# A two-layer transformer forward pass on one core: the 32-row block exchange moved from GpSimd's to SyncE's queue, the first x tiles loaded in halves, and the chunk states computed alternately in two banks

## The chip, the cores and the metric

The kernel runs on one core of a Trainium2 chip. The metric is the device time of one execution in microseconds (us), lower is better. TensorE is PE in the profile (PEld are its weight loads), VectorE is DVE, ScalarE ACT, GpSimd POOL, SyncE SP.

## The reference

Two transformer blocks over 256 tokens of width 2048, in float32. The first has an attention with a forget gate and a feed-forward network with a causal convolution of width 3. The second has gated linear attention (GLA, 4 heads, chunks of 64 tokens) and dilated attention (8 heads) side by side, and a gated feed-forward network of width 5632. Cut to what matters here:

```
def first_block(x, ...):
    h = x
    a = rms_norm(h, mix_norm)
    h = h + fox_mixer(a, ...)            # 16 heads: softmax(q k^T * scale + cum_i - cum_j) v, then @ w_out
    return h + conv_ffn(rms_norm(h, ffn_norm), ...)

def second_block(x, ...):
    h = rms_norm(x, norm1_g)
    qa, ka, va, ra, ga, qb, kb, vb = split(h @ w_in)
    mix = concat([gla_mixer(qa, ka, va, ra, log_g), dilated_mixer(qb, kb, vb)])
    x = x + mix @ w_out
    h2 = rms_norm(x, norm2_g)
    return x + (silu(h2 @ w_gate) * (h2 @ w_up)) @ w_down

# in gla_mixer, per head and chunk n of 64 tokens:
chunk_state[n] = k_dec[n]^T @ v[n]                      # 128 x 256
state[n] = decay[n] * state[n-1] + chunk_state[n]
```

## The kernel before, in words

**Products.** Every large product `x @ w` is made by `gemm` for one block of 512 output columns at a time. Weights come in tiles of 1 MB (4 x 128 input rows by 512 columns). `dma_to` loads them on SP's queue into `raw`, which has three buffers (NRAW). `split_to` turns half a tile (a unit) into a rounded high part `wh` (ACT, L105) and the rest `wl` (DVE, L111), in five buffers (NSPL), four units ahead of the product (LEAD). Each unit is 12 matmuls of 128x512 on PE (L118 to L120: high by high, low by high, high by low, for two blocks of 128 tokens and two of 128 input rows). A block with 2048 input rows is 8 units, 96 matmuls.

**Order.** Everything is written out in program order, engine by engine: after each unit `gemm` calls `pump`, which advances generators by one `yield`. An evacuation (`resid`, `plain`, `conv_evac`, `up_evac`) is such a generator; attention and GLA (`attention`, `gla`) run in a second list. Each engine works through its instructions in that order, and the splits of `split_to` stand four units ahead of PE's products among them.

**Block exchange.** Products give tokens on partitions, and the next product needs features there. Where `flip` is used, DVE first transposes blocks of 32x32 (`turn`, L312); one `yield` later `exchange` writes `turn` to DRAM in four stores of 128 KB (`way`, L303); another `yield` later one load of 512 KB brings it back with the blocks exchanged (L318). Four yields later ACT reads the result (L328). `turned` does the same for two heads' attention weights (`pturn`). These DMAs are issued by POOL. POOL also puts the residual `h` away to DRAM and fetches it (`home`), loads the gate sums (`cum_dram`, `ckb`) and does part of the head norms (L241, L242, L392) and of the attention bias (L656 to L661).

**Residual blocks.** `resid` adds the product to `h` (DVE, L347), and for the first three of four blocks flips it and splits it for the next product (`r`, L105 and L111). The fourth block is transposed by PE (`tp`, L290). On ACT and DVE the split of block n's flip stands ahead of the add of block n + 1.

**Start.** x comes transposed in four tiles of 512 KB (`xr`), each scaled and split into `x` by `prep_x` (ACT L107, DVE L113) before the weight units that use it. Tile 0 is loaded and prepared in quarters. For tiles 1 to 3 `load_x` fetches the whole tile ahead of its weight tile.

**Chunk states.** In `gla`, for n = 0, 1, 2, four float32 matmuls (one per head) with 64 rows of contraction make `cs`; n = 0 and n = 2 use partitions 0 to 63 of `kd` and `v`, n = 1 partitions 64 to 127. Each n is one step of the pump, with two PSUM tiles of two heads each.

Of the kernel before, what the change touches and what calls it, by code (L numbers as in the profile page):

```python
# [18 lines left out]
P = 128  # L19
D = 2048  # L20
S = 256
# [22 lines left out]
def fox_gla_dilated_kernel(  # L44
# [36 lines left out]
    def alloc(shape, dt, name):  # L81
        i = free_slots.popleft()
        t = slots.tile([P] + shape, dt, tag=f"s{i}", name=name)
        slot_of[id(t)] = (i, t)
        return t
# [53 lines left out]
    def dma_to(i):  # L139
        while next_dma[0] <= min(i, len(plan) - 1):  # L140
            k = next_dma[0]
            t = rawp.tile([P, 4, 512], F32, tag="raw", name="raw")
            src = plan[k].rearrange("p (k c) -> p k c", c=512)
            if k == 0:
                for q in range(4):
                    nc.sync.dma_start(out=t[:, q], in_=src[:, q])
            else:
                if k < KG:
                    load_x(k)
                if k < 3:  # L150
                    for q in (slice(0, 2), slice(2, 4)):
                        nc.sync.dma_start(out=t[:, q], in_=src[:, q])
                else:
                    nc.sync.dma_start(out=t, in_=src)
                if k == 3:
                    nc.sync.dma_start(out=cols[:, C_FFN:], in_=cols_d[:, C_FFN:])
                    nc.sync.dma_start(out=wn, in_=w_n.rearrange("p (a k c) -> p a k c", a=2, c=16))
                if k == 8:
                    nc.sync.dma_start(out=const, in_=const_d)
                if 4 <= k < 8:  # L160
                    fetch(k - 4, nc.sync)
            raw_t[k] = t
            next_dma[0] += 1

    def split_to(u, mid=None):
        while next_spl[0] <= min(u, 2 * len(plan) - 1):
            k = next_spl[0]
            dma_to(k // 2 + NRAW - 1)
            if k in (2, 4, 6):
                prep_x(k // 2)  # L170
            r = raw_t[k // 2][:, (k % 2) * 2:(k % 2) * 2 + 2]
            wh = splp.tile([P, 2, 512], F32R, tag="wh", name="wh")
            wl = splp.tile([P, 2, 512], F32R, tag="wl", name="wl")
            if k < 2:
                for q in range(2):
                    if mid:
                        mid(2 * k + q)
                    hi_of(wh[:, q], r[:, q])
                    lo_of(wl[:, q], r[:, q], wh[:, q])
            else:  # L180
                hi_of(wh, r)
                lo_of(wl, r, wh)
            spl_t[k] = (wh, wl)
            if k % 2:
                raw_t.pop(k // 2)
            next_spl[0] += 1
# [81 lines left out]
    wn = cpool.tile([P, 2, 16, 16], F32, name="wn")  # L268
    gqk = cpool.tile([P, 2], F32, name="gqk")

    def load_x(i, kt=None):
        src = x_t[i].rearrange("p (k c) -> p k c", c=S)
        if kt is None:
            nc.sync.dma_start(out=xr[i], in_=src)
        else:
            nc.scalar.dma_start(out=xr[i][:, kt], in_=src[:, kt])

    rows = {}

# [20 lines left out]
    def exchange(turn, width):  # L300
        way = ways.tile([P, 4, S], F32, tag="way", name="way")
        for i in range(4):
            nc.gpsimd.dma_start(out=way[:, i, 0:width].rearrange("(j c) e -> c j e", c=32),  # L303
                              in_=turn[32 * i:32 * i + 32, :, 0:width])
        return way[:, :, 0:width]

    def flip(src, into=None):
        turn = alloc([4, S], F32, "turn")
        sv = src.rearrange("p t (k q c) -> p t q k c", q=4, c=32)
        qv = turn.rearrange("p q (k t r) -> p t q k r", t=2, r=32)  # L310
        for t in range(2):
            dve.transpose(out=qv[:, t], in_=sv[:, t])  # L312
        yield
        way = exchange(turn, S)
        yield
        held = alloc([4, S], F32, "flip") if into is None else into
        f = held.rearrange("p a c -> p (a c)").rearrange("p (i e) -> p i e", i=4)
        nc.gpsimd.dma_start(out=f, in_=way)  # L318
        for _ in range(4):
            yield  # L320
        return f.rearrange("p i (k t r) -> p k t i r", k=4, t=2), held, turn
# [93 lines left out]
    def attention(box, gqk, bias_of, ot, done, tag, flipped, ready=None):  # L415
# [58 lines left out]
        def turned(pairs):  # L474
            held = {}
            for a in pairs:
                turn = alloc([4, S], F32, "pturn")
                for n in range(2):
                    pb = sm.pop(a + n)
                    dve.transpose(  # L480
                        out=turn[:, :, n * 96:(n + 1) * 96].rearrange("p j (c r) -> p j c r", c=3),
                        in_=pb[:, 0].rearrange("p (c j r) -> p j c r", c=3, j=4),
                    )
                    free(pb)
                yield
                way = exchange(turn, 192)
                yield
                held[a] = turn
                nc.gpsimd.dma_start(out=turn[:, :, 0:192], in_=way)
            for _ in range(3):  # L490
                yield
            for a in pairs:
                f = held[a][:, :, 0:192].rearrange("p i (n c r) -> p n c i r", n=2, c=3)
                for n in range(2):
                    pt[a + n] = alloc([3, P], F32, "pts")
                    act.copy(pt[a + n].rearrange("p c (i r) -> p c i r", i=4), f[:, n])
                free(held[a])
                yield
# [36 lines left out]
    def run_all():  # L535
# [287 lines left out]
        def gla():  # L823
# [34 lines left out]
            while "v1" not in G:  # L858
                yield
            v = [G["v0"], G["v1"]]  # L860
            st = []
            for n in range(3):
                t, r0 = n // 2, (n % 2) * 64
                s_ = alloc([4, S], F32, "state")
                for pr in range(2):
                    ps = side([2, S], "cs")
                    for kk in range(2):
                        hd = pr * 2 + kk
                        pe.matmul(ps[:, kk], kd[r0:r0 + 64, t, hd * P:(hd + 1) * P],
                                  v[pr][r0:r0 + 64, t, kk * S:(kk + 1) * S], start=True, stop=True)  # L870
                    if n == 0:
                        act.copy(s_[:, pr * 2:pr * 2 + 2], ps)
                    else:
                        for kk in range(2):
                            hd = pr * 2 + kk
                            dve.scalar_tensor_tensor(
                                out=s_[:, hd], in0=st[-1][:, hd], scalar=eb[:, hd, n * 64 + 63:n * 64 + 64],
                                in1=ps[:, kk], op0=ALU.mult, op1=ALU.add)
                st.append(s_)
                yield  # L880
            free(kd)
            o = [alloc([2, 512], F32, f"o{i}") for i in range(2)]
            ssq = small.tile([P, 2, 4], F32, tag="ssq", name="ssq", bufs=1)
# [209 lines left out]
```

## Time and profile before

| | |
|---|---|
| time, median of 3 runs | 2243.42 us (2242.3 to 2247.32) |
| the profiled execution's own time | 2246.22 us |
| its span, first to last instruction | 2244.4 us |
| mean granted TensorE clock | 0.997 |
| PE busy | 2219.1 us (99%) |
| DVE, ACT, POOL busy | 1290.0, 1148.9, 316.3 us |
| DMA: SP's queue (q1), POOL's queue (q0), share of 16 engines | 53.3%, 11.5% |

The last DMA of the span is not part of it, which leaves 1.8 us between the span and the time. PE's busy time counts a matmul from its start to its modelled end, so overlapping matmuls hide short gaps. Where the profile says "DMA to landing", it counts from the issue of a DMA to its last byte's semaphore. The clock is 1.00 for 2.4 GHz and 0.50 for 1.2 GHz.

### The profile page before, as it was taken

How to read it: one execution, taken by the hardware profiler on the slowest of the kernel's cores; microseconds unless marked ns; L12 is line 12 of the kernel's file. 1: busy time of each engine (PE TensorE's matmuls, PEld its weight loads, DVE VectorE, ACT ScalarE, POOL GpSimd, SP SyncE). 2: the span in 40 equal slices, each digit the busy share in tenths (PEclk: the TensorE clock that was granted, in tenths of full speed). 3: DMA queues.
4: the chain of work that ended last, by engine and by line, in shares of the span. 5: the costliest groups of instructions: out<-in, count | busy, mean ns of one | idle time of the engine just before them, and what ended most of it. 6: DMA issues, size and time to landing. Idle time of an engine off the chain costs nothing.

```text
span 2244.4 us, 25865 instructions
## 1 busy us (share of the span) xinstructions
PE 2219.1 (99%) x9888; PEld 1827.7 (81%) x9888; DVE 1290.0 (57%) x1531; ACT 1148.9 (51%) x1565; POOL 316.3 (14%) x483
## 2 busy tenths in 40 slices
PE   9999999899999999999999999999999999999999
PEld 6788888788888888888887887887888888888887
DVE  5656565466767677654555663555555555554443
ACT  6555555466666656544456654544444444444332
POOL 0453321011111111000222320010000000000000
PEclk9999999999999999999999999999999999999999
DMA  7676657677777777666664773585666666676553
GB/s 297 234 252 209 226 194 245 226 234 252 234 242 243 240 245 245 221 232 236 235 217 168 253 250 135 204 279 193 227 217 212 217 225 214 210 245 228 197 203 116
DMA packets 87403, 502.27 MB, mean 224 GB/s; under 512 B 12560, under 2 KB 14272, under 8 KB 37488
## 3 DMA queue, kind: packets, MB, share of 16 engines
q1 hardware_dynamic: 60272, 417.59, 53.3%
q0 software_dynamic: 26144, 82.39, 11.5%
q8 instruction: 77, 1.26, 0.2%
q10 hardware_dynamic: 864, 0.66, 0.1%
q14 instruction: 46, 0.38, 0.1%
HBM read 459.94 MB, written 40.65 MB: 223 GB/s over the span
## 4 chain that ended last, share of the span: by engine, by line
PE 91%; DMA 4%; ACT 1%; POOL 1%; DVE 1%; issue 1%; ACTq 0%; DVEq 0%; POOLq 0%; SPq 0%
PE acc L118 29%; PE acc L120 29%; PE acc L119 29%; DMA way<-turn 2%; DMA flip<-way 1%; POOL way L303 1%; ACT wh L105 1%; PE sc L443 0%; DMA xr<-in_x_t_dram 0%; DMA way<-pturn 0%; ACT turn L328 0%; PE nar L603 0%; DMA ckb<-cum_dram 0%; DVE h L347 0%; PE sc L442 0%
## 5 line engine op out<-in xcount | busy, mean ns | idle before, releaser
L111 DVE TENSOR_TENSOR wl<-raw,wh 128x1024 fp32r<-128x1024 f32 (+1 forms) x786 | 964.6, 1230 | 816.8 <-ACT wh L105 816.3
L105 ACT CAST wh<-raw 128x1024 fp32r<-128x1024 f32 (+1 forms) x786 | 820.5, 1048 | 793.3 <-PE acc L120 758.7
L118 PE MATMUL acc<-wh,r 128*128 128x512 f32 x1792 | 702.1, 392 | 0.0
L120 PE MATMUL acc<-wh,r 128*128 128x512 f32 x1792 | 698.1, 390 | 0.0
L119 PE MATMUL acc<-wl,r 128*128 128x512 f32 x1792 | 698.0, 390 | 0.0
L118 PEld LDWEIGHTS acc<-wh,r 128*128 128x128 f32 x1792 | 337.1, 188 | 72.0 <-issue 2.5
L120 PEld LDWEIGHTS acc<-wh,r 128*128 128x128 f32 x1792 | 336.8, 188 | 70.5
L119 PEld LDWEIGHTS acc<-wl,r 128*128 128x128 f32 x1792 | 336.9, 188 | 69.3
L118 PE MATMUL acc<-wh,g 128*128 128x512 f32 x704 | 273.9, 389 | 0.0
L119 PE MATMUL acc<-wl,g 128*128 128x512 f32 x704 | 273.9, 389 | 0.0
L120 PE MATMUL acc<-wh,g 128*128 128x512 f32 x704 | 273.9, 389 | 0.0
L303 POOL DMA_DIRECT2D way<-turn x216 | 119.5, 560 | 984.0 <-DVE turn L312 909.0
L118 PE MATMUL acc<-wh,x 128*128 128x512 f32 x384 | 154.5, 402 | 1.2 <-ACT wh L105 1.2
L120 PEld LDWEIGHTS acc<-wh,g 128*128 128x128 f32 x704 | 132.1, 188 | 27.6
L119 PEld LDWEIGHTS acc<-wl,g 128*128 128x128 f32 x704 | 132.1, 188 | 27.5
L118 PEld LDWEIGHTS acc<-wh,g 128*128 128x128 f32 x704 | 132.1, 188 | 27.3
L119 PE MATMUL acc<-wl,x 128*128 128x512 f32 x384 | 149.8, 390 | 0.8 <-DVE wl L111 0.8
L120 PE MATMUL acc<-wh,x 128*128 128x512 f32 x384 | 150.0, 391 | 0.0
L118 PEld LDWEIGHTS acc<-wh,x 128*128 128x128 f32 x384 | 72.4, 189 | 16.6 <-ACT wh L105 1.6
L119 PEld LDWEIGHTS acc<-wl,x 128*128 128x128 f32 x384 | 72.5, 189 | 15.9 <-DVE wl L111 1.3
L120 PEld LDWEIGHTS acc<-wh,x 128*128 128x128 f32 x384 | 72.2, 188 | 15.7
L714 DVE SCALAR_TENSOR_TENSOR u<-turn,cols,u 128x255 f32<-128x255 f32 (+1 forms) x176 | 80.9, 481 | 3.1
(212 smaller groups left out, 1470.0 us busy)
## 6 DMA issues: line engine op xcount, KB each, us to landing
raw<-in_w_dram SPq DMA_DIRECT2D x301, 1024.0 KB, 5.0
raw<-in_w7g_dram SPq DMA_DIRECT2D x44, 1024.0 KB, 4.8
raw<-in_w7u_dram SPq DMA_DIRECT2D x44, 1024.0 KB, 5.0
way<-turn POOLq DMA_DIRECT2D x216, 128.0 KB, 4.7
u<-way POOLq DMA_DIRECT2D x22, 512.0 KB, 5.0
home<-h POOLq DMA_DIRECT2D x12, 512.0 KB, 6.6
h<-home POOLq DMA_DIRECT2D x12, 512.0 KB, 8.4
sg<-way POOLq DMA_DIRECT2D x11, 512.0 KB, 5.6
```

Source lines behind the costliest of these rows:

```text
L105: act.copy(out_, in_)
L111: dve.tensor_tensor(out=out_, in0=in_, in1=hi.bitcast(F32), op=ALU.subtract)
L118: pe.matmul(out_, xh, wh, start=first, stop=False)
L119: pe.matmul(out_, xh, wl, start=False, stop=False)
L120: pe.matmul(out_, xl, wh, start=False, stop=last)
L303: nc.gpsimd.dma_start(out=way[:, i, 0:width].rearrange("(j c) e -> c j e", c=32), in_=turn[32 * i:32 * i + 32, :, 0:width])
L714: dve.scalar_tensor_tensor(out=yy[:, d:S], in0=n[:, kt, 0:S - d], scalar=col(C_CW + 176 - 88 * d + ch), in1=yy[:, d:S], op0=ALU.mult, op1= ...
```

## The change

Three edits. The five DMAs of a block exchange (in `exchange`, `flip` and `turned`) are issued by SP instead of POOL. For x tiles 1 and 2 the load is cut in two halves of 256 KB, each issued just ahead of the half of the weight tile that it is used with, and `prep_x` prepares tiles 1 to 3 in halves, each ahead of its unit. In `gla` the states of chunks 0 and 1 are computed together, head by head, alternating between two PSUM tiles, and chunk 2 follows; the pump is still given three steps.

```
             else:
-                if k < KG:
-                    load_x(k)
                 if k < 3:
                     for q in (slice(0, 2), slice(2, 4)):
+                        load_x(k, q, nc.sync)
                         nc.sync.dma_start(out=t[:, q], in_=src[:, q])
                 else:
+                    if k < KG:
+                        load_x(k)
                     nc.sync.dma_start(out=t, in_=src)
...
-            if k in (2, 4, 6):
-                prep_x(k // 2)
+            if 2 <= k < 8:
+                prep_x(k // 2, (0, 1) if k % 2 == 0 else (2, 3))
...
     def exchange(turn, width):
...
-            nc.gpsimd.dma_start(out=way[:, i, 0:width].rearrange("(j c) e -> c j e", c=32),
+            nc.sync.dma_start(out=way[:, i, 0:width].rearrange("(j c) e -> c j e", c=32),
...
-        nc.gpsimd.dma_start(out=f, in_=way)
+        nc.sync.dma_start(out=f, in_=way)
...
-                nc.gpsimd.dma_start(out=turn[:, :, 0:192], in_=way)
+                nc.sync.dma_start(out=turn[:, :, 0:192], in_=way)
...
-            for n in range(3):
-                t, r0 = n // 2, (n % 2) * 64
-                s_ = alloc([4, S], F32, "state")
-                for pr in range(2):
-                    ps = side([2, S], "cs")
-                    for kk in range(2):
-                        hd = pr * 2 + kk
-                        pe.matmul(ps[:, kk], kd[r0:r0 + 64, t, hd * P:(hd + 1) * P],
-                                  v[pr][r0:r0 + 64, t, kk * S:(kk + 1) * S], start=True, stop=True)
...
+            def chunk(ps, n, pr, kk):
+                t, r0, hd = n // 2, (n % 2) * 64, pr * 2 + kk
+                pe.matmul(ps[:, kk], kd[r0:r0 + 64, t, hd * P:(hd + 1) * P],
+                          v[pr][r0:r0 + 64, t, kk * S:(kk + 1) * S], start=True, stop=True)
...
+            for pr in range(2):
+                two = [side([2, S], "cs") for _ in range(2)]
+                for kk in range(2):
+                    for n in range(2):
+                        chunk(two[n], n, pr, kk)
+                act.copy(st[0][:, pr * 2:pr * 2 + 2], two[0])
+                carry(two[1], 1, pr)
+                yield
+            for pr in range(2):
+                ps = side([2, S], "cs")
+                for kk in range(2):
+                    chunk(ps, 2, pr, kk)
+                carry(ps, 2, pr)
+            yield
```

Where the instructions now stand. POOL's queue before the change, where the first attention begins (`q`, `k`: the first group's queries and keys):

```order
L392 TENSOR_TENSOR k<-k,rsh 128x1024
L303 DMA way<-turn 32x4x256 x4
L643 DMA cum_dram<-cumts 16x256
L647 DMA ckb_613<-cum_dram 128x1024
L647 DMA ckb_615<-cum_dram 128x1024
L647 DMA ckb_617<-cum_dram 128x1024
L647 DMA ckb_619<-cum_dram 128x1024
L318 DMA q<-way 128x1024
L303 DMA way<-turn 32x4x256 x4
L318 DMA k<-way 128x1024
```

SP's queue after the change at the same place:

```order
L155 DMA raw<-in_w_dram 128x2048 x4
L304 DMA way<-turn 32x4x256 x4
L155 DMA raw<-in_w_dram 128x2048
L319 DMA q<-way 128x1024
L304 DMA way<-turn 32x4x256 x4
L155 DMA raw<-in_w_dram 128x2048
L319 DMA k<-way 128x1024
```

The exchange of q and k no longer stands behind the gate sums; each exchange now has one 1 MB weight load between its stores and its load back.

SP's queue after the change at the end of the second block's output projection (`flip`: a residual block):

```order
L155 DMA raw<-in_w_dram 128x2048 x3
L304 DMA way<-turn 32x4x256 x4
L155 DMA raw<-in_w_dram 128x2048
L319 DMA flip<-way 128x1024
L155 DMA raw<-in_w_dram 128x2048 x2
L155 DMA raw<-in_w7g_dram 128x2048
L304 DMA way<-turn 32x4x256 x4
L155 DMA raw<-in_w7g_dram 128x2048
L319 DMA flip<-way 128x1024
```

Before the change SP's queue held only the weight loads here, and the `way` and `flip` rows stood on POOL's, in the same order.

PE in the chunk states before (the number behind `cs` is the PSUM tile; the first two of the three steps):

```order
L869 MATMUL cs_10569<-v0_10375,kd_10434 128x256 x2
L869 MATMUL cs_10573<-v1_10545,kd_10434 128x256 x2
L869 MATMUL cs_10594<-v0_10375,kd_10434 128x256 x2
L869 MATMUL cs_10599<-v1_10545,kd_10434 128x256 x2
```

And after, the first of the three steps:

```order
L866 MATMUL cs_10573<-v0_10377,kd_10436 128x256
L866 MATMUL cs_10574<-v0_10377,kd_10436 128x256
L866 MATMUL cs_10573<-v0_10377,kd_10436 128x256
L866 MATMUL cs_10574<-v0_10377,kd_10436 128x256
```

Neighbours now differ in the half of the partitions that they read and in the PSUM tile that they write.

## Rows read from the trace of the kernel before

**Rows 1.** Stretches: length; busy (count) PE, PEld, DVE, ACT, POOL; clock, DMA share, GB/s.

```profile
10.00:40.00 30.00, 28.04 (x123) 21.67 (x122) 19.80 (x26) 19.99 (x33) 0.00 (x0) 1.00 1.02 407
408.40:413.40 5.00, 4.84 (x16) 3.99 (x17) 3.54 (x6) 2.30 (x6) 0.54 (x1) 0.54 0.81 301
1530.00:1900.00 370.00, 370.00 (x1634) 306.39 (x1633) 199.08 (x202) 164.68 (x186) 22.10 (x40) 1.00 0.64 217
```

**Rows 2.** Waits, whole run: who waited for whom; total us, times, longest.

```profile
ACT turn L328 <- DMA q<-way: 13.8, 2, 12.0
PE tp L290 <- DVE h L347: 12.2, 3, 7.6
PE sc L442 <- ACT turn L328: 5.6, 1, 5.6
```

**Rows 3.** Chain that ended last, pieces in order of time: start us, us, what.

```profile
95.82 0.80 PE sc L442 x2
...
97.47 0.43 PE acc L118
...
409.03 1.75 PE tp L290 x7
...
1129.97 0.87 PE tp L290 x8
...
1475.83 1.22 DVE turn L312 x2
...
1492.00 1.71 ACT turn L328 x4
...
1496.87 1.28 DVE h L347 x2
...
1499.28 1.22 DVE turn L312 x2
...
1525.35 0.43 PE acc L120
```

**Rows 4.** DVE's timeline, 62 to 98 us: start, us, instruction, idle before.

```profile
65.35 1.29 DVE L312 STREAM_TRANSPOSE turn<-q 128x512 f32<-128x512 f32 x2
...
70.51 1.29 DVE L312 STREAM_TRANSPOSE turn<-k 128x512 f32<-128x512 f32 x2
```

**Rows 5.** POOL's timeline, same stretch.

```profile
76.98 0.53 POOL L318 DMA_DIRECT2D q<-way  x1
...
81.59 0.55 POOL L303 DMA_DIRECT2D way<-turn  x1 [2.41 <-DMA ckb<-cum_dram]
```

**Rows 6.** DMA issues, whole run: queue, count, KB each, median us to landing.

```profile
out_dram<-h SPq DMA_DIRECT2D x7, 256.0 KB, 2.2
```

**Rows 7.** The weight loads of line 154, 600 to 700 us.

```profile
L154 SPq DMA_DIRECT2D raw<-in_w_dram x18: 327/328/328, 605.1 to 697.9; - x18
...
DMA to landing us min/median/max: 4.7/6.1/7.9
```

**Rows 8.** Chain that ended last, at the start.

```profile
5.15 6.59 DMA xr<-in_x_t_dram
11.77 1.71 ACT x L107 x4
```

**Rows 9.** PE's timeline at the start, 12.4 to 16 us, with idle before.

```profile
14.46 0.49 PE L118 MATMUL acc<-wh,x 128*128 128x512 f32 x1 [1.19 <-ACT wh L105]
15.72 0.50 PE L119 MATMUL acc<-wl,x 128*128 128x512 f32 x1 [0.76 <-DVE wl L111]
```

**Rows 10.** PE's timeline at GLA, 1369 to 1387 us.

```profile
1369.64 1.99 PE L869 MATMUL cs<-v,kd 64*128 64x256 f32 x8
1371.56 0.50 PE L118 MATMUL acc<-wh,r 128*128 128x512 f32 x1
...
1384.36 0.43 PE L891 MATMUL o<-v,at 128*64 128x256 f32 x1
...
1386.24 0.50 PE L118 MATMUL acc<-wh,r 128*128 128x512 f32 x1
```

More of the change, by code (lines that the diff above doesn't have):

```diff
@@ L269, in fox_gla_dilated_kernel, with load_x @@
     gqk = cpool.tile([P, 2], F32, name="gqk")
-    def load_x(i, kt=None):
+    def load_x(i, kt=None, queue=nc.scalar):
         src = x_t[i].rearrange("p (k c) -> p k c", c=S)
@@ L275, in load_x @@
         else:
-            nc.scalar.dma_start(out=xr[i][:, kt], in_=src[:, kt])
+            queue.dma_start(out=xr[i][:, kt], in_=src[:, kt])
     rows = {}
@@ L860, in gla, with carry @@
             v = [G["v0"], G["v1"]]
-            st = []
-            for n in range(3):
-                t, r0 = n // 2, (n % 2) * 64
-                s_ = alloc([4, S], F32, "state")
-                for pr in range(2):
-                    ps = side([2, S], "cs")
-                    for kk in range(2):
-                        hd = pr * 2 + kk
-                        pe.matmul(ps[:, kk], kd[r0:r0 + 64, t, hd * P:(hd + 1) * P],
-                                  v[pr][r0:r0 + 64, t, kk * S:(kk + 1) * S], start=True, stop=True)
[L871 to L879, printed above, removed]
-                yield
+            st = [alloc([4, S], F32, "state") for _ in range(3)]
+            def chunk(ps, n, pr, kk):
+                t, r0, hd = n // 2, (n % 2) * 64, pr * 2 + kk
+                pe.matmul(ps[:, kk], kd[r0:r0 + 64, t, hd * P:(hd + 1) * P],
+                          v[pr][r0:r0 + 64, t, kk * S:(kk + 1) * S], start=True, stop=True)
+            def carry(ps, n, pr):
+                for kk in range(2):
+                    hd = pr * 2 + kk
+                    dve.scalar_tensor_tensor(
+                        out=st[n][:, hd], in0=st[n - 1][:, hd], scalar=eb[:, hd, n * 64 + 63:n * 64 + 64],
+                        in1=ps[:, kk], op0=ALU.mult, op1=ALU.add)
+            for pr in range(2):
[5 more added lines that the diff above has]
+                carry(two[1], 1, pr)
+                yield
+            for pr in range(2):
+                ps = side([2, S], "cs")
+                for kk in range(2):
+                    chunk(ps, 2, pr, kk)
+                carry(ps, 2, pr)
+            yield
             free(kd)
```

## The prediction

> **What bounds the kernel now.** I read the page first, then the windows, the waits, and the chain of waits at each place where PE stands still. The table of the profile has PE busy 99% of the span; in a stretch without a stall 1634 matmuls take 370 us, 0.2264 us each at full clock [rows 1]. So a block of 96 matmuls takes 21.7 us and a unit of 12 takes 2.72 us, and nothing helps that doesn't shorten PE's own work or one of its few waits. The list of waits has two that matter: `tp` waits 12.2 us for the residual add, almost all in two places (7.6 us the longest), and the first `sc` waits 5.6 us for a turned operand [rows 2]. At the start PE waits 1.2 and 0.8 us more [rows 9]. That is all: 19.8 us. What follows a long wait is slow too: after the stall at 400 us the granted clock is 0.54 over 5 us [rows 1], and seven transposes take 1.75 us where eight take 0.87 elsewhere [rows 3].
>
> **The residual blocks (two output projections).** The chain shows a loop that goes round once per residual block. DVE ends the transposes of one at 1475.83 + 1.22 = 1477.05; the blocks are stored and loaded back, and ACT reads them at 1492.00: 15.0 us. From there to the next block's add it is 4.9 us (1496.87: ACT and DVE do the split first), and to the end of the next transposes 3.6 us more (1499.28 + 1.22 = 1500.50) [rows 3]. Together 23.5 us, against 21.7 us of PE's work for a block. So each of three exchanges puts the adds further behind, until PE waits for the last one. The stall goes when exchange and read take less than 21.7 - 4.9 - 3.6 = 13.2 us.
>
> What does SP's queue make of the 15.0? Issuing: four stores at 0.33 us, as SP's loads take [rows 7], 1.3 us. Landing of the stores: at best 2.2 us, as a 256 KB store on SP [rows 6]; at worst they stand behind a whole 1 MB load (4.7 us, the shortest in [rows 7]) and take their own time, 512 KB at 407 GB/s = 1.3 us [rows 1]: 6.0 us. The load back: at best 2.2 + 0.6 for twice the bytes = 2.8 us, at worst again behind the weight load that now stands between, 6.0 us. With two handovers of 0.3 us: 6.9 to 13.9 us. I take 10: at the stores the load ahead has mostly landed (it waits for the DVE split that runs before the transposes), at the load back it has not. That is 18.5 us a round, under 21.7, and only the very top of the range is over it. So both stalls go: 12.2 us.
>
> **The first attention.** Here the order on POOL's queue is late, not the transfer. q's transposes end at 65.35 + 1.29 = 66.6 [rows 4], but POOL issues q's load only at 76.98, after 2 MB of `ckb`, and one store of k waits 2.41 us more for `ckb` [rows 5]. ACT stands 12.0 us at q's load [rows 2], and k's read, on which `sc` hangs, is late. After the change q and k stand on SP between weight loads. q lands by some 66.6 + 10 = 77; k's transposes end at 71.8 [rows 4], plus 10, plus what `ckb` takes from a shared 407 GB/s (at most 2 MB, 5.2 us): 82 to 87, then ACT's four reads, 1.7 us. PE comes to `sc` at 95.82 - 5.6 = 90.2 [rows 2, 3], or 89 with the gain at the start. This fits, with 0.5 to 5 us to spare: 5.6 us. The bounds are 0 (if weights, `ckb` and both exchanges fill the DMAs until 90) and 5.6.
>
> **The clock.** After each of the three stalls PE runs at the lower level for some us. In the chain 11 matmuls there (first at 97.47, last at 1525.35) take 0.43 us in place of 0.23: 2.2 us; the two sets of transposes lose 7 x (0.25 - 0.11) = 1.0 us each [rows 3]. That is 4.2 us, and it goes with the stalls. The bounds are 0 and three times the 5 x 0.46 = 2.3 us that [rows 1] makes of one stall, 6.9.
>
> **The start.** x's tile 1 lands at 5.15 + 6.59 = 11.74, then four ACT operations take 1.71 us before the first weight cast [rows 8]. DMA is full there at 407 GB/s [rows 1], so 512 KB are 1.3 us: half of x lands at 11.1, the first weight half at 12.4 (13.0 before), and two ACT operations are done at 12.0. The cast takes 1.0 us, DVE's rest 1.26 us more (14.46 to 15.72), and L119 starts at 14.7 in place of 15.72 [rows 9]. Gain 1.0 us; between 0.4 (weights land as before) and the whole 2.0. Two more issues on SP cost nothing as long as bytes wait in the queue, which a full DMA shows.
>
> **Chunk states.** One step is 8 records in 1.92 us, 0.24 each (1369.64 to 1371.56); in `o`, whose matmuls alternate between two halves of the output partitions, 12 records take 1.88 us, 0.16 each (1384.36 to 1386.24) [rows 10]. So halves overlap; there it is columns of the array, here it would be rows, which no row of the profile shows. If they do, two of three steps fall to half: 1.9 us less; if not, 0. I take 1.7, since `o` shows it in one direction. "TensorEngine Tiling (Array Packing)" of the Trainium skill, Key Properties, has tiles work independently, and its Gotcha 1 asks for different PSUM banks of different row tiles, which the edit gives; by it the sum would have 1.9. ACT's copy and the carries on DVE stay and have two steps of the pump, 5 us, until `o` needs them.
>
> **What it may cost.** SP now waits in order: behind each load back (until its stores have landed) stands the next weight load. A weight load is issued when the tile three before it is split, 12.4 us ahead of its own split by the code (two tiles of 5.44 us and some 1.5); it lands after 4.7 to 7.9 us [rows 7], so 4.5 to 7.7 us are spare. The split itself runs four units, 10.9 us, ahead of PE and takes 2.3: 8.6 more. I count 15 us of cover. An exchange makes SP wait some 4 us for its stores and puts 1 MB (2.6 us) before weights: under 7 us. With two exchanges in one block (`pturn` and q) it is some 9. It is covered, so 0.
>
> **Sum.** 2246.22 - 12.2 - 5.6 - 4.2 - 1.0 - 1.7 = 2221.5 us, against the profiled execution's own time, which is 2.8 us above the median of the runs shown. On the median's footing 2218.7; I add 1.3 us for short waits that will show where the long ones were (a `tp` that comes just before its add): **2220 us**. This case's own range is 2214 to 2227.
>
> **Rivals.**
> (a) *Part of it stays.* In the first attention the DMAs are too full, or one output projection still stalls. For: `ckb`, two exchanges and the weights fall together. Against: the time to spare. It gives 2220 + 5.6 + 1 (clock) = 2227 or, with the longer `tp` wait, 2220 + 7.6 + 1.5 = 2229; with both 2236.
> (b) *The queue makes no difference.* The exchange takes 15 us on SP as well (stores behind a load, load back behind a load, the top of my range and a little more), and only the start, the chunk states and the order at the first attention help. For: the bytes and the 16 DMA engines stay the same. Against: the direct order. 2220 + 12.2 + 3.4 = 2236, and 2243 if the first attention stays too.
> The Trainium skill's "DMA: Bandwidth & Descriptors", Issuing engines are not separate DMA queues, says that DMAs of all issuers run on the same engines and interleave, so that another issuer saves only the issue time. By it alone (b) is what happens; the trace agrees that the engines are shared, but q's load at 76.98 [rows 5] is late by the order within a queue, which the rule leaves open.
> (c) *Slower: SP's waits starve the weights.* The place is the groups with two kinds of exchange (four groups of three blocks, 65.2 us each). There q1 must carry 12 MB of weights and 3.5 MB of exchanges, 15.5 x 2.56 = 39.7 us, and SP waits 8 times. If the queue runs dry for L us at each, a group takes 39.7 + 8 L, more than 65.2 from L = 3.2. Two such groups follow each other, twice, with 15 us of cover: the loss is 2 x (2 x (8 L - 25.5) - 15) = 32 L - 132 us, which eats the gain of 25 at L = 4.9. At L = 5.5 it is 44 us: 2220 + 44 = 2264. Against: the weight load between stores and load back keeps the queue filled, and a store alone lands after 2.2 us [rows 6], so that L is nearer 2.
>
> **Chances.** Forecast 0.62; (a) 0.17; (b) 0.10, of which 0.05 within 0.2%; (c) 0.11, of which 0.01 ends within 0.2% and the rest above. 0.2% (4.5 us) is about what a measurement of this kernel can tell from no change. Faster: 0.62 + 0.17 + 0.05 = 0.84, less 0.01 for what I have not seen, which goes to no change; same 0.05 + 0.01 + 0.01 = 0.07; slower 0.10. The range leaves out (c), the slow end of (b) and a few hundredths below: 2213 to 2240.
>
> **What would show it.** In the profile after: no wait of `tp` for `h` and of `sc` for `turn` above 1 us, and a clock of 1.00 throughout; from the end of a residual block's transposes to ACT's read near 10 us, surely under 13; ACT's wait for q's load under 3 us; the first L119 after the start's wait at 14.7; each of the first two chunk steps near 1.0 us. Wrong would be: waits of ACT's casts for `raw`, followed by PE's for `wh`, in the attention groups (c), or exchanges of 15 us with the same `tp` waits (b).

## The result, and the profile after

The changed kernel takes 2218.05 us (median of 4 runs, 2217.24 to 2218.59) where the kernel before takes 2245.08 us beside it (2242.3 to 2247.32): a ratio of 0.988, 95% interval 0.9863 to 0.9897. 2220 was predicted. The profiled execution took 2218.33 us, its span is 2216.6 us.

The page of the kernel after (busy time of the engines, the granted clock, the queues, and one row of DMA issues):

```profile
PE 2210.6 (100%) x9888; PEld 1823.4 (82%) x9888; DVE 1294.0 (58%) x1531; ACT 1153.9 (52%) x1565; POOL 135.2 (6%) x163
...
PEclk9999999999999999999999999999999999999999
...
q1 hardware_dynamic: 110480, 482.09, 63.2%
q0 software_dynamic: 4960, 17.88, 2.1%
...
way<-turn SPq DMA_DIRECT2D x216, 128.0 KB, 2.8
```

PE is all but full, POOL fell from 316.3 to 135.2 us of work, and its queue from 11.5% to 2.1% of the DMA engines. Now the waits, PE's and then the new ones on SP (who waited for whom; total us, times, longest):

```profile
PE warm L572 <- DVE warm L569: 1.4, 1, 1.4
PE acc L119 <- DVE wl L111: 0.8, 1, 0.8
```

```profile
SPq L304 <- DVE turn L313: 180.5, 49, 5.2
SPq L319 <- DMA way<-turn: 104.1, 99, 3.0
...
SPq L490 <- DMA way<-pturn: 27.5, 21, 5.2
```

Nothing answers to the `tp` and `sc` rows of [rows 2]: both waits are gone, and what PE still waits for lies at the start. L319 loads back 54 exchanges (216 stores, four each), and the 99 are waits for single stores, so SP stands still for its stores some 1.9 us per load back (104.1 in 54). Ahead of the stores it also stands 180.5 us, until DVE's transposes are done. The stretches that answer to [rows 1], the second of them at the end of the first output projection, now at 390 us (length; busy and count of PE, PEld, DVE, ACT, POOL; clock, DMA share, GB/s):

```profile
10.00:40.00 30.00, 29.17 (x127) 22.30 (x126) 20.10 (x27) 20.13 (x34) 0.00 (x0) 1.00 1.03 403
...
389.60:394.60 5.00, 5.00 (x27) 4.22 (x27) 3.48 (x6) 1.76 (x5) 0.56 (x1) 1.00 0.77 275
```

The clock there was 0.54 before and is 1.00. Where the time went can be read off more sharply than from any one row. Both kernels start 9408 matmuls into `acc` in the same order, so the start of the n-th in the one trace less its start in the other is the gain up to that point of the program. Taken at the same places for every kernel with a profile (each against the one profiled execution of before, in us; e1 to e12 are the experiments below):

| kernel | start, to 25 | first attention, to 105 | to 400 | first output projection, to 420 | feed-forward and second attention, to 1360 | chunk states, to 1380 | second output projection, to 1530 | all |
|---|---|---|---|---|---|---|---|---|
| after | 1.5 | 7.3 | 0.4 | 10.1 | 0.0 | 1.8 | 6.5 | 27.7 |
| e1 exchange alone | -1.7 | 7.3 | 0.4 | 10.1 | 0.0 | 0.0 | 6.5 | 22.7 |
| e2 x halves alone | 1.5 | -0.9 | 0.1 | 1.6 | -1.0 | 0.0 | -1.2 | 0.0 |
| e3 chunk states alone | 1.6 | -1.5 | 0.3 | 1.2 | -0.5 | 1.8 | -3.2 | -0.2 |
| e4 residual blocks alone | -1.4 | -0.3 | 0.2 | 10.1 | 0.0 | 0.0 | 6.5 | 15.1 |
| e5 after, x whole | 0.6 | 7.3 | 0.4 | 10.1 | 0.0 | 1.8 | 6.5 | 26.8 |
| e6 after again | 1.9 | 7.3 | 0.4 | 10.1 | 0.0 | 1.8 | 6.5 | 28.1 |
| e7 finer start | 2.5 | 7.0 | 0.4 | 10.1 | 0.0 | 1.8 | 6.5 | 28.3 |
| e8 stores on GpSimd | -1.5 | 2.0 | 0.4 | 10.1 | 0.0 | 0.0 | 6.5 | 17.6 |
| e9 stores on ScalarE | 0.9 | 7.3 | 0.4 | 9.6 | 0.0 | 0.0 | 6.0 | 24.2 |
| e10 bias tiles on SyncE | 0.9 | 1.0 | -0.6 | 1.3 | -1.3 | 0.0 | -1.2 | 0.2 |
| e11 before, two raw | 1.3 | -4.4 | -1.0 | 1.7 | -8.6 | 0.0 | -1.1 | -12.0 |
| e12 after, two raw | 1.0 | 3.0 | 0.2 | 4.3 | -0.2 | 1.8 | -0.9 | 9.1 |

Two things are to be seen before any experiment is told. Where a stall is wholly gone, its column repeats to 0.1 us from kernel to kernel (but for e7's 7.0); where it stays (e2, e3, e10 in the output projections), it differs by 1 to 3 us from execution to execution. And the start differs by up to 3 us among kernels whose start is the same code (x whole: -1.7 to 1.6). Part of this is the clock and not the transfers: in e1, e4 and e8 the granted clock falls behind the start's short waits, in the kernel before, after and the others with three raw tiles it doesn't. The stretch from 15 to 20 us (columns as above), before and in e1:

```profile
15.00:20.00 5.00, 4.28 (x19) 3.55 (x20) 5.00 (x8) 4.66 (x9) 0.00 (x0) 1.00 1.02 419
```

```profile
15.00:20.00 5.00, 4.25 (x12) 3.35 (x13) 5.00 (x8) 4.63 (x9) 0.00 (x0) 0.66 1.02 421
```

A clock of 0.66 over 5 us costs 5 x 0.34 = 1.7 us, an estimate from that row; it is about what the three have in their first column (-1.7, -1.4, -1.5).

The places themselves. First the residual loop that [rows 3] shows, here round its third block in the first output projection (timelines of SP, ACT, DVE and PE: start, us, instruction, what ended the idle time before):

```profile
370.22 1.30 DVE L313 STREAM_TRANSPOSE turn<-h 128x512 f32<-128x512 f32 x2
...
371.54 2.12 SPq L304 DMA_DIRECT2D way<-turn  x4
...
376.25 0.34 SPq L319 DMA_DIRECT2D flip<-way  x1
...
383.49 1.05 ACT L105 CAST wh<-raw 128x1024 fp32r<-128x1024 f32 x1 [1.67 <-PE acc L120]
384.44 1.71 ACT L329 ACTIVATE turn<-flip,cols 128x256 f32<-128x256 f32 x4
...
389.31 1.28 DVE L348 TENSOR_TENSOR h<-acc,h 128x512 f32<-128x512 f32 x2
...
391.45 1.03 PE L291 MATMUL tp<-const,h 128*128 128x128 f32 x8
```

The load back, in the DMA view of the 0.5 us round its issue (KB, us from issue to landing):

```profile
flip<-way SPq DMA_DIRECT2D x1, 512.0 KB, 5.3
```

The transposes end at 371.52, the data is back at 376.25 + 5.3 = 381.5: 10.0 us, where [rows 3] has 15.0 to ACT's read. ACT reads it at 384.44 and not at once, for it comes there in its own order: the cast at 383.49 had waited for PE, and the read follows it. So there were 2.9 us to spare here. The eight transposes of `tp` stand right behind the adds, without a wait. The start and the chunk states, answering to [rows 9] and [rows 10]:

```profile
12.95 0.50 PE L118 MATMUL acc<-wh,x 128*128 128x512 f32 x1
...
14.20 0.50 PE L119 MATMUL acc<-wl,x 128*128 128x512 f32 x1 [0.76 <-DVE wl L111]
...
1350.26 1.14 PE L866 MATMUL cs<-v,kd 64*128 64x256 f32 x8
1351.32 0.50 PE L118 MATMUL acc<-wh,r 128*128 128x512 f32 x1
...
1358.27 1.99 PE L866 MATMUL cs<-v,kd 64*128 64x256 f32 x8
1360.19 0.51 PE L118 MATMUL acc<-wh,r 128*128 128x512 f32 x1
```

A step of alternating halves takes 1.06 us from its first record to the product behind it, the third step, one half alone, 1.92 as before.

### The profile page after: what moved, and what is told of

It is laid out like the page before. It is cut to its first block, busy times and chain, and to the rows that moved or that the text cites. A ratio compares the mean times of both kernels' runs of the same rounds, so it can differ in the third digit from the quotient of the medians.

```text
span 2216.6 us, 25859 instructions
## 1 busy us (share of the span) xinstructions
PE 2210.6 (100%) x9888; PEld 1823.4 (82%) x9888; DVE 1294.0 (58%) x1531; ACT 1153.9 (52%) x1565; POOL 135.2 (6%) x163
## 4 chain that ended last, share of the span: by engine, by line
PE 99%; DMA 0%; DVE 0%; ACT 0%; ACTq 0%; DVEq 0%; issue 0%
PE acc L118 32%; PE acc L120 32%; PE acc L119 32%; PE sc L444 0%; PE nar L604 0%; DMA raw<-in_w_dram 0%; PE sc L443 0%; PE ov L508 0%; PE ov L507 0%; PE ov L506 0%; PE tp L291 0%; DMA cols<-in_cols_dram 0%; PE cs L866 0%; PE o L908 0%; PE o L903 0%; PE narow L614 0%
## 5 line engine op out<-in xcount | busy, mean ns | idle before, releaser
L118 PE MATMUL acc<-wh,r 128*128 128x512 f32 x1792 | 702.0, 392 | 0.0
L119 PE MATMUL acc<-wl,r 128*128 128x512 f32 x1792 | 698.1, 390 | 0.0
L118 PEld LDWEIGHTS acc<-wh,r 128*128 128x128 f32 x1792 | 336.7, 188 | 71.4 <-issue 2.5
L119 PEld LDWEIGHTS acc<-wl,r 128*128 128x128 f32 x1792 | 336.7, 188 | 68.9
L119 PE MATMUL acc<-wl,g 128*128 128x512 f32 x704 | 274.2, 389 | 0.0
L118 PE MATMUL acc<-wh,g 128*128 128x512 f32 x704 | 274.2, 389 | 0.0
L118 PEld LDWEIGHTS acc<-wh,g 128*128 128x128 f32 x704 | 132.2, 188 | 27.4
L119 PEld LDWEIGHTS acc<-wl,g 128*128 128x128 f32 x704 | 132.2, 188 | 27.3
L118 PE MATMUL acc<-wh,x 128*128 128x512 f32 x384 | 154.1, 401 | 0.1
L119 PE MATMUL acc<-wl,x 128*128 128x512 f32 x384 | 149.8, 390 | 0.8 <-DVE wl L111 0.8
L119 PEld LDWEIGHTS acc<-wl,x 128*128 128x128 f32 x384 | 72.3, 188 | 15.9 <-DVE wl L111 1.6
L118 PEld LDWEIGHTS acc<-wh,x 128*128 128x128 f32 x384 | 72.2, 188 | 15.3 <-ACT wh L105 0.7
L261 POOL DMA_DIRECT2D h<-home x12 | 6.7, 554 | 918.0 <-issue 455.1
```

What stands on the lines that cost most here:

```text
L118: pe.matmul(out_, xh, wh, start=first, stop=False)
L119: pe.matmul(out_, xh, wl, start=False, stop=False)
L261: queue.dma_start(out=h[c], in_=home[c])
```

## The experiments

The theory: the stalls came from the exchange on POOL's queue, from the order in it and from its slow transfers beside the weights, and the queue carries some 22 of the 27 us. The rival: x halves and chunk states, or the parts together, carry much of it.

**e1, the exchange alone on SyncE.**

```
 kernel before, with
-  nc.gpsimd.dma_start(way <- turn), (flip <- way), (turn <- way)
+  nc.sync.dma_start(the same five)
```

> The kernel before with the block exchange alone moved to SyncE's queue (stores, load back, and the load back of the softmax tiles); x whole, chunk states one after the other. Theory: the queue carries 12.2 + 5.6 + 4.2 = 22.0 us of the gain, so some 22 below the kernel before of the same chip (about 2223), some 3 to 4 above the kernel after; the waits of tp for h and of sc for turn are gone and the granted clock is 1.00 at 409 us and at 1500 us. Rival: x halves and chunk states bear more than their 2.7 us, or the three parts only work together; then this one gains 15 us or less, and a wait of tp or sc is left.

Measured: 2220.92 us, ratio 0.9891 (0.9876 to 0.9905) to a before of 2246.33: 25.4 us less. No wait of `tp` or `sc` is left in the profile, and the three stalls give back 7.3, 10.1 and 6.5 us, to 0.1 us what they give in the kernel after. The theory holds; the gain is even 3.4 us above its number. (The table's 22.7 is less because the profiled execution, 2223.43 us, is the longest of four; its mean clock is 0.999, for the stretch at the start, and that of the other three 1.000.)

**e2, x halves alone, and e3, chunk states alone.** The first takes the hunks on `load_x` and `prep_x` of the diff, the second that on `gla`, and both leave the exchange on POOL.

> The kernel before with x in halves with their weight halves alone. Theory: L119 of the second tile starts 1.0 to 1.5 us earlier than 15.72 us, and the span is shorter by this: 1.0 to 1.5 us, under what the times can tell. Rival: the 1 us is given back at the first wait of sc, because what it waits for stands on the other queue and doesn't move with PE; then L119 is earlier, the wait of sc 1 to 1.5 us longer, and the span the same.

> The kernel before with the chunk states of two halves alternating alone. Theory: the matmuls of two row halves overlap, the first two steps' eight records take about 1 us each in place of 1.92, and the span is 1.7 us shorter. Rival: they don't overlap, and the gain seen in the kernel after is from elsewhere; 1.92 us a step for the same records and 0 us.

Measured: 2245.84 us (ratio 1.0002, 0.9993 to 1.0011) and 2245.07 us (0.9992, 0.9979 to 1.0006): neither can be told from no change. In the traces both do what they should: L119 starts at 14.24, and the chunk states gain 1.8 us in the table. But with x whole e3 itself has L119 at 14.11, so an early start in one execution proves nothing; and what either gains is less than the differences of the stalls behind it (e2 loses 0.9 and 1.2 in two of them, e3 1.5 and 3.2). Whether a stall takes back such a gain by rule or by chance isn't settled by one profile each.

**e4, the residual blocks alone.**

```
-  f, held, turn = yield from flip(h[cb])                    # all of flip on POOL
+  f, held, turn = yield from flip(h[cb], queue=nc.sync)     # in resid only
```

> The kernel before with the exchange of the residual blocks alone on SyncE's queue (six exchanges, three in each output projection); q, k, softmax tiles and all else stay on GpSimd's. Theory: the two tp stalls (12.2 us) and two of the three stretches at the lower clock (2.8 us) go, and the sc wait of 5.6 us stays: 15 us below the kernel before, about 2230. Rival: the first attention delays all that comes behind it, or the residual stalls come from what else lies on GpSimd's queue (the stores and loads of h); then less than 8 us.

Measured: 2229.97 us (0.9929, 0.9914 to 0.9944), 16.4 us less than before. Both columns of the output projections are those of the kernel after (10.1 and 6.5), and `sc` still waits, 5.8 us. The edit moves nine exchanges and not six: `resid` also ends the first block's feed-forward, where no stall stood and nothing was gained (0.0 in that column). So the six of the output projections carry two thirds of the gain of e1; the first attention carries the rest, 9.1 us by the medians of e1 and e4.

**e5, e6, e7: the start without the stalls behind it.** e5 is the kernel after with x whole, e6 the kernel after itself. e7 goes on where the change stopped:

```
-                    for q in (slice(0, 2), slice(2, 4)):
+                    for q in range(4) if k == 1 else (slice(0, 2), slice(2, 4)):
...
-            if k < 2:                    # weight casts in quarters
+            if k < 4:
...
-                    if mid:
+                    if k > 1:
+                        prep_x(1, (2 * k - 4 + q,))
+                    elif mid:
...
-                for t, kk in sorted(pairs, key=lambda p: p[1]) if u < 2 else pairs:
+                for t, kk in sorted(pairs, key=lambda p: p[1]) if u < 4 else pairs:
```

> The kernel after, but with x loaded and prepared whole, as before (exchange on SyncE's queue, chunk states alternating). With the long stalls gone nothing behind the start can take back what the start gains. Theory: x halves are worth 1.0 to 1.5 us, so this one ends 1.0 to 1.5 us above the kernel after, with L119 of the second tile 1.0 to 1.5 us later than in it. Rival: the start's transfers differ by as much from one execution to the next (L119 at 14.1 us in one execution with x whole, at 15.7 us in four), and the medians differ by under 0.5 us.

> The kernel after itself, beside the other runs on this chip. Both theories: about 2218 us; its profile shows which of the start's times repeat (L119 at 14.2 us) and which differ between executions.

> The kernel after with the second tile's x, weights and casts in quarters, and its matmuls in the order in which the quarters come. Theory: what is left of the start's stall, 0.50 us at L118 and 0.76 us at L119, goes: 1.3 us below the kernel after, about 2217. Rival: four more DMA issues delay the landings behind them by as much as the finer casts give; then within 0.5 us of the kernel after.

Measured: 2219.16 us (2217.93 to 2219.68), 2218.36 us (2217.9 to 2218.63) and 2218.05 us (2217.95 to 2218.34). The medians say 0.8 us for x halves, between theory and rival, and the ranges overlap. The L119 of tile 1 in e5 and e6 (one row of each timeline):

```profile
15.14 0.50 PE L119 MATMUL acc<-wl,x 128*128 128x512 f32 x1 [0.77 <-DVE wl L111]
```

```profile
13.78 0.50 PE L119 MATMUL acc<-wl,x 128*128 128x512 f32 x1 [0.51 <-DVE wl L111]
```

Over all profiles with three raw tiles L119 starts at 13.78, 14.20 and 14.24 with halves, and with x whole at 14.11 (e3), 14.80, 14.84, 15.14 and four times between 15.65 and 15.75. So halves help by about 1 us, and the start's own spread is larger. Of the four with the latest L119, three (e1, e4, e8) lose the 1.7 us to the clock besides; none of the kernels with halves does, and whether halves always prevent it is not shown by four profiles. In e7 PE waits at neither row, as its theory said, and gains 0.6 to 1.0 us up to 25 us against e6 and after; 0.3 to 0.4 of that is gone by the end of the first attention, and 0.3 us of median is nothing that these runs can tell. No version beats the kernel after measurably: PE has hardly a wait left to take away. What the chunk states are worth without the stalls can be read here too: e5 is e1 with them, and its median is 1.8 us below e1's, with ranges that don't overlap, though the two were not measured beside each other.

**e8 and e9: which half of the exchange is slow on POOL, and is it POOL?** Both start from the kernel before and put the load back on SP. The stores stay on POOL in e8 and go to ACT's queue in e9.

```
-  nc.gpsimd.dma_start(out=f, in_=way)          # and turn <- way
+  nc.sync.dma_start(out=f, in_=way)
   e9 also:
-  nc.gpsimd.dma_start(out=way..., in_=turn...)
+  nc.scalar.dma_start(out=way..., in_=turn...)
```

> The kernel before with the load back on SyncE's queue and the four stores left on GpSimd's. Theory: it is the stores that are slow there (8.3 to 10.4 us from the end of the transposes to the last landing in the residual blocks before, 4.6 to 7.5 after), because they share the DMA engines with weight loads that were issued behind them; so the stores still take 8 us or more, the exchange 14 us or more, both tp stalls stay, and the time is within 8 us of the kernel before (2237 to 2246). Rival: the load back made the difference; then the exchange takes 10 to 13 us and the time is near that of the exchange wholly on SyncE's queue, 2221.

> The kernel before with the four stores of an exchange on ScalarE's queue and the load back on SyncE's. With the stores on GpSimd's queue and the same load back they took 8.8 to 9.1 us in the residual blocks, with all on SyncE's 4.5 to 8.3. Theory: a store beside weight loads of another queue is slow whoever issues it, since both share the 16 DMA engines packet by packet; so 8 us or more here too, exchanges of 12 to 14 us, no tp stall (this is near the 13.2 us that a round has), and the sc wait gone too, since ScalarE's queue has no bias tiles ahead of k's stores: 2221 to 2225, the upper end if ScalarE's waits for the transposes delay its casts. Rival: it is GpSimd's queue that is slow; then the stores take 3 to 5 us, the exchange 7 to 10 us, and the time is near 2221.

Measured: 2224.87 us (0.9914, 0.9899 to 0.9928) and 2220.95 us (0.9893, 0.9876 to 0.9909). e8 overturns the time that I gave it and not what I said of the stores. DMA views of the third residual block of the first output projection, at the issue of its stores and of its load back, in e8:

```profile
raw<-in_w_dram SPq DMA_DIRECT2D x1, 1024.0 KB, 7.3
way<-turn POOLq DMA_DIRECT2D x4, 128.0 KB, 5.8
...
flip<-way SPq DMA_DIRECT2D x1, 512.0 KB, 4.5
```

and in e9:

```profile
raw<-in_w_dram SPq DMA_DIRECT2D x1, 1024.0 KB, 8.3
way<-turn ACTq DMA_DIRECT2D x4, 128.0 KB, 8.1
...
flip<-way SPq DMA_DIRECT2D x1, 512.0 KB, 3.5
```

In all six residual blocks the last store lands 8.8 to 9.1 us after the transposes in e8 and 7.9 to 10.3 in e9, against 4.5 to 8.3 in e1. So stores beside weight loads of another queue are slow whether POOL or ACT issues them: POOL as such is not the cause. But the load back gains what the stores lose. SP can't issue weights while it waits for the stores, so the load back meets less beside it (in the block shown the weights ahead have landed 0.5 us before its issue in e8, in e1 5.5 us after it), and lands after 3.2 to 4.9 us (e8), 3.6 to 4.1 (e9), against 4.8 to 6.7 in e1 and 5.3 to 7.1 before. Together that is 12.1 to 13.8 us in e8 and 12.0 to 14.4 in e9. The prediction's threshold was 13.2, and just here a `tp` wait comes back, of 0.5 us in e9 and none in e8. The Trainium skill's "DMA: Bandwidth & Descriptors", Issuing engines are not separate DMA queues, has the DMAs of all issuers interleave on the same engines. The slow stores agree, and e9 ends where e1 does (2220.95 and 2220.92). The other half alone, stores on SP and load back on POOL, was not run.

What keeps e8 above e1 is the first attention: k's stores still stand behind `ckb` on POOL (issued at 78.46, landed at 90.8), and `sc` waits 3.4 us.

**e10, only the bias tiles off POOL.**

```
-                pool.dma_start(out=ckb[g], in_=sc...)
+                nc.sync.dma_start(out=ckb[g], in_=sc...)
```

> The kernel before, all exchanges on GpSimd's queue as before, with only the four loads of the bias tiles (ckb, 2 MB) issued by SyncE. Theory: the first attention's stall is the order on GpSimd's queue; q's load and k's stores no longer stand behind ckb, so q's load is issued within 1 us of its stores' landing and the sc wait of 5.6 us goes, with the clock's 1.4 us behind it: 2238, and both tp stalls stay. Rival: the queue's own transfers are too slow beside weights and ckb; q and k land no earlier than before, and the time is within 2 us of the kernel before.

Measured: 2244.57 us (0.9998, 0.9982 to 1.0013): nothing. Its waits of PE:

```profile
PE acc L118 <- ACT wh L105: 2.7, 2, 2.5
...
PE sc L442 <- ACT turn L328: 1.0, 1, 1.0
```

and the DMA views at 73.2 to 76.3 us and at k's load back:

```profile
ckb<-cum_dram SPq DMA_DIRECT2D x4, 512.0 KB, 7.0
raw<-in_w_dram SPq DMA_DIRECT2D x2, 1024.0 KB, 13.6
q<-way POOLq DMA_DIRECT2D x1, 512.0 KB, 7.8
way<-turn POOLq DMA_DIRECT2D x4, 128.0 KB, 8.3
...
k<-way POOLq DMA_DIRECT2D x1, 512.0 KB, 7.8
```

q's load is issued 0.6 us after its stores' landing, as the theory said, and it lands at 81.5 in place of 89.6; the first attention's `sc` doesn't wait any more (the row of 1.0 is an `sc` at 1278 us, in the second attention). But k's stores (transposes done at 70.9, issued at 74.27 behind q's load) take 8.3 us among 2 MB of `ckb` and the weights, and the weights, now behind `ckb`, land after 13.6: the stall goes to L118, which waits 2.5 us, and the granted clock is 0.50 from 89 to 95.5 us behind it. Order alone was not the cause of this stall.

**e11 and e12: the cover against SP's waits.** `NRAW = 2` in place of 3, in the kernel before and in the kernel after.

> The kernel before with two raw weight tiles in place of three, as the reference for the same in the kernel after. Both theories: a weight load is issued one tile (5.44 us) later, some 7 us ahead of its split against landings of 4.7 to 7.9 us; the split's own 8.6 us cover it, so within 2 us of the kernel before.

> The kernel after with two raw weight tiles in place of three: its cover against SyncE's waits falls from some 15 us to some 9.6. Theory: an exchange costs the weights 7 us, two in one block 9; that is still covered, and it ends within 4 us of the kernel after (2218 to 2222), with more of ScalarE's waits for raw tiles than the 13 us of the kernel after. Rival (c): SyncE's waits starve the weights once cover is short; then PE waits for wh in the attention groups, and it loses 10 us or more against the kernel after, which the same edit doesn't cost the kernel before.

Measured: 2251.09 us (1.0024, 1.0008 to 1.004) and 2242.11 us (0.9985, 0.9974 to 0.9997). The kernel before loses 5.8 us, the kernel after 24: nearly all of its gain. Both theories missed, e11's of within 2 us and e12's of within 4. The size in e12 is the rival's (10 us or more), but neither theory nor rival had the place. e12's waits of PE and of ACT:

```profile
PE tp L291 <- DVE h L348: 8.5, 3, 4.8
PE acc L119 <- DVE wl L111: 1.7, 3, 0.8
```

```profile
ACT wh L105 <- DMA raw<-in_w_dram: 380.3, 141, 7.7
```

and its timeline round the last residual block of the first output projection (ACT, then DVE and PE):

```profile
389.93 2.00 ACT L105 CAST wh<-raw 128x1024 fp32r<-128x1024 f32 x2 [5.95 <-DMA raw<-in_w_dram]
393.65 1.05 ACT L105 CAST wh<-raw 128x1024 fp32r<-128x1024 f32 x1 [1.72 <-DMA raw<-in_w_dram]
394.60 1.70 ACT L329 ACTIVATE turn<-flip,cols 128x256 f32<-128x256 f32 x4
...
399.46 1.28 DVE L348 TENSOR_TENSOR h<-acc,h 128x512 f32<-128x512 f32 x2
...
400.20 0.33 PE L291 MATMUL tp<-const,h 128*128 128x128 f32 x1 [3.49 <-DVE h L348]
```

The flip is back at 391.1, 10.9 us after the transposes that end at 380.2. But ACT works in order: its casts ahead of the read wait 5.95 and 1.72 us for weights that stand behind the exchange on SP's queue, so the read comes at 394.60, 14.4 us after the transposes, the add at 399.46, and `tp` waits again. The splits still reach PE nearly in time (1.7 us of waits); what is late is what ACT does behind them. In the table 13.2 of the 18.6 us that e12's profile lies behind the kernel after are lost in the two output projections. Another 4.3 are lost by 53 us, before the first exchange: two raw tiles also delay the load of `const`, for which `narow` waits 1.6 us in e12 and 4.4 in e11, with a lower clock behind it. (The profiled execution, 2236.89 us, is the shortest of e12's ten.)

## Why the prediction came out as it did

**The time**: 2218.05 against 2220, on the side of more gain. The sum was 24.7 us; the traces differ by 27.7, the medians by 27.0. Against the 2243.42 shown then, 2220 was a gain of 23.4; that the time came out nearer than the gain is luck, since the median of before rose by 1.7 us, to 2245.08. The terms that missed are the clock (1.9 too little) and the short waits (1.3 too much).

**Residual blocks**: right in mechanism, shown by e4. The waits of 12.2 us went. An exchange of "10" is 10.0 to 13.6 us in the six blocks of the kernel after (1476.19 to 1487.07 is 10.9), inside the range of 6.9 to 13.9. The loop was mis-drawn in one point: ACT's read was put at the landing, but ACT comes to it in its order, at 12.9 us in the block shown and at 13.3 to 13.8 in the other five. So the sign that the prediction named, a read "surely under 13", failed in five of six blocks without a stall: the round is set by PE (21.8 to 22.3 us from transposes to transposes), and the reserve lies between landing and read. The prediction also left out that `resid` ends the feed-forward; there a round has 59.8 us, and no stall. The threshold of 13.2 is right to some tenths: e8 and e9 lie on it, and one exchange of 13.6 in the kernel after passes without a wait.

**First attention**: the stall went, and k landed at 85.3, inside 82 to 87, q at 74.8 where 77 was said. But the sentence that "the order on POOL's queue is late, not the transfer" failed: e10 took `ckb` out of that order and gained nothing, because 2 MB beside k's stores delay them as much as 2 MB ahead of q's load. The trace of the kernel before had shown that the transfer is slow too: q's load takes 12.6 us from its issue at 76.98, where the median of the six `q` loads is 6.6:

```profile
q<-way POOLq DMA_DIRECT2D x1, 512.0 KB, 12.6
```

What counts is that k's stores leave ahead of `ckb`: at 70.34 in the kernel after, and at 71.34 in e9, where the stall is gone too although they go over ACT's queue; in e8 they leave at 78.46, and 3.4 us of it stay.

**Clock**: mis-sized. Over the three stalls the table has 7.3, 10.1 and 6.5, 23.9 us, of which 17.8 are the waits themselves [rows 2]; 6.1 is left for what follows them, where the sum had 4.2 and the bound 6.9. The 11 matmuls and two sets of transposes that the sum counted from the chain were not all that the lower level cost. The granted clock behind the first and the third stall (columns as above), beside the 0.54 that [rows 1] has behind the second:

```profile
95.80:100.80 5.00, 4.98 (x16) 4.10 (x17) 4.00 (x10) 4.78 (x10) 5.00 (x9) 0.68 0.90 333
...
1522.10:1527.10 5.00, 4.71 (x18) 3.95 (x19) 3.55 (x6) 2.29 (x6) 0.54 (x1) 0.66 0.78 267
```

That is 5 x (0.32 + 0.46 + 0.34) = 5.6 us, an estimate from these rows, and most of the 6.1.

**Start**: 1.0 predicted; 1.5 in the profile, 0.8 by the medians of e5 and e6. The profiles alone would have misled, since the landing of the first transfers, and the clock behind the start's waits, differ by more than that.

**Chunk states**: 1.7 predicted, 1.80 in every trace that has the edit. Row halves do overlap, and fully but for 0.06 us a step (half of 1.92 is 0.96, and 0.90 is gained). The Trainium skill's "TensorEngine Tiling (Array Packing)", Key Properties, has tiles work independently, which makes 1.9, an estimate; the traces agree to 0.1 us.

**Cost of SP's waits**: 0 was right, and by less than I thought. I counted 15 us of cover against 7 to 9; one buffer fewer, a cover of 9.6 by the same count, costs 24 us (5.8 in the kernel before, which has no such waits). What failed is the way to count: cover was taken up to PE's need of `wh`, while ACT's reads of the exchange stand in line behind the casts, and these have only the raw tiles' lead. Rival (c) was thus nearer than its 0.11 with "starved weights" said, and by another path: its L, the wait per load back, is some 1.9 us for those of `flip` and 2.8 for `pturn` (27.5 in ten), near the 2 that the prediction took and under the 4.9 that would have eaten the gain. Not counted at all were SP's 180.5 us at the stores, for the transposes; three raw tiles cover these too.

**Residual short waits**: the 1.3 us added to the sum for them don't exist; no `tp` wait shows in the kernel after.

**Rivals (a) and (b)** didn't come. (b) failed since an exchange on SP takes 10 to 13.6 us and not 15; e8 and e9 show how near the edge lies.

## What to carry to other kernels

In a kernel like this one, a round trip through DRAM beside a stream of large loads is best tried in the queue of that stream, ahead of the next load, if the stream has a spare buffer to pay for the issuer's waits; the load back matters most (with the stores on ACT's queue e9 is as fast). Measure that reserve by taking a buffer away. Count the reserve for everything that stands in line behind the buffered work on its engine, not for the last consumer alone. And a gain of 1 us ahead of a stall that differs by 1 to 3 us can't be measured until the stall is gone: remove the stall first, then judge the small edits.

## What the runs showed of the hardware

Two queues on the same DMA engines don't share as one would like for a latency: while the 0.52 MB of one exchange's stores went out on POOL's queue (1477.0 to 1485.6 us of the kernel before), weights moved three and a half times as much (packets, MB, share of 16 engines):

```profile
q1 hardware_dynamic: 253, 1.81, 65.5%
q0 software_dynamic: 192, 0.52, 20.7%
```

All but some 0.2 MB of these weights were issued at 1478.18 and 1482.07, after the first store (1477.34); the first of the two loads landed at 1485.39, the last store at 1485.58. In the weights' own queue the same four stores are down after 4.5 to 8.3 us (e1). There the next weight load also leaves only behind the fourth store, so that order and sharing are not told apart. That the issuer is hardware or software made no difference to this (8.8 to 9.1 us from POOL, 7.9 to 10.3 from ACT), though the packets on ACT's and SP's queues are smaller (e9's page has 32.92 MB in 37728 packets on ACT's queue, against the 0.52 MB in 192 here); the median landing of all 128 KB stores is 4.7 us from POOL, 3.0 from ACT and 2.8 from SP. What else might set the share of a queue, the size of its packets say, no run here varied alone.
